# Decode step of the gated attention spread among the last gate projections, chunk 0's readout begun amid them, fourth plain weight in two tiles

## The chip, the cores and the metric

One core of one Trainium2 chip runs the whole step in one launch. The metric is the device time of that launch in microseconds; the profile is of one execution, and the times of the runs stand beside it.

## The reference

A decoder step of two layers for a prompt of 1024 tokens and 8 decode tokens, model width 1024. Cut to what this change touches, layer 0 is:

```python
h = rmsnorm(x, norm_mix_pre[l])
q, k, v, r, glr, qm = split_cols(h @ w_in_a[a], IN_A_SIZES)
g = log_sigmoid(glr @ w_gate_up[a] + b_gate[a]) / 16
o, S = gla_recurrence(q, k, v, g, gla_state[a])     # 4 heads, state 96 x 192 each
o_main = rmsnorm(o, gla_norm[a]) * silu(r)
o_mem = mem_attend(qm, mem_k[l], mem_v[l])
x = x + rmsnorm(concat([o_main, o_mem]) @ w_out[l], norm_mix_post[l])
f = square(relu(rmsnorm(x, norm_ffn_pre[l]) @ w_ffn_up[l])) @ w_ffn_down[l]
x = x + rmsnorm(f, norm_ffn_post[l])
```

For the 8 decode tokens the recurrence is a single step per head and token: the old state (an input, one per token) times exp(g), plus the outer product of k and v, is the new state (an output), and q times it is the token's o.

## The kernel before

The activations lie transposed, model width on partitions, and the 1032 tokens (1024 prompt, 8 decode) are three chunks of 384, 384 and 264 columns; the decode tokens are the last columns of chunk 2. Every float32 operand of a projection is split into a high and a low part (ScalarE's cast writes the high, VectorE's subtraction the low), and a projection of one 128-wide output block of one chunk, a *unit*, is 8 slices of the model width times three matmuls: high weight by high x, high by low, low by high, 24 in all (`proj`, lines 240 to 250). A unit's result is in one PSUM bank (tiles `mm`, `mx`); four banks go round.

Layer 0's mixer ends as follows. `in_r` (lines 1240 to 1265) runs the gate projections: for each unit VectorE takes the PSUM bank into a temporary `t` (L1257), clamps it (L1258), ScalarE takes exp, ln and exp (L1259 to L1261), VectorE makes r * silu(r) of it in three steps (L1262 to L1264), and SP's queue stores it to `srd` in DRAM (L1265). Blocks 0 to 2 run earlier, amid the prompt's recurrence. Blocks 3, 4 and 5, nine units, run last, chunk by chunk, with temporaries from a pool `gt` of four buffers.

The decode step of the recurrence stands in the program ahead of these nine units. For each of 4 heads SP loads the states `sin` and, broadcast, the v rows `vb`; for each of 8 tokens ScalarE scales a state (L1570) and VectorE adds k times v (L1571); SP stores the new states (L1572); 8 matmuls read them out into a PSUM tile `sf` or `sx` (L1577, 16 records, as each float32 matmul is recorded twice), and VectorE copies that to `vdec` (L1579). Then `vdec` is normed.

`out_proj` (from L487) follows: for chunk c, `make_o0` loads `srd` back (tile `sr`, L1592), transposes the recurrence's result block by block with TensorE (tile `ot`, two PSUM banks, L1595, 18 transposes for a 384-column chunk), multiplies both on VectorE (L1599) and splits the product into the operand `oh`/`ol` (records `xh<-sr`, `xl<-sr`). That operand lies in the buffers which chunk c of the layer's input had. Then 8 units per chunk with the weights `w_out`; the first three weights lie in the three buffers that hold the gate weights before.

The MLP (`mlp`, from L610) starts with four plain output blocks, m = 0 to 3, of each chunk (`up_plain`); three weights lie in the pool `wA`, the fourth (tile `wx`, both halves in one tile) in a pool `w4` on the side where the output weights lay.

A scheduling layer sets the order on each engine from the program's order, priorities and its own costs; engines then run their queues in order. So a step that moves in the program moves on five queues.

Of the kernel before, what the change touches and what calls it, by code (L numbers as in the profile page):

```python
# [8 lines left out]
F32 = mybir.dt.float32  # L9
F32R = mybir.dt.float32r  # L10
# [6 lines left out]
P = 128  # L17
D = 1024
KT = 8
# [9 lines left out]
DV = 192  # L29
# [4 lines left out]
NPL = 4  # L34
# [13 lines left out]
def hybrid_decoder_step(ctx: ExitStack, tc: tile.TileContext, A, O):  # L48
    nc = tc.nc
# [40 lines left out]
    def nm(s):  # L90
        uid[0] += 1
        return f"{s}_{uid[0]}"
# [35 lines left out]
    def stps(tag=None):  # L128
        turn[1] ^= 1
        tag = tag or ("sf", "sx")[turn[1]]  # L130
        return pst.tile([P, 512], F32, tag=tag, name=nm(tag))
# [105 lines left out]
        nc.gpsimd.tensor_tensor(ws, ws, gains[:, g, :].unsqueeze(2).to_broadcast([P, KT, P]), ALU.mult)  # L237
        nc.gpsimd.dma_start(wfd[i], ws)

    def proj(ps, w, hl, n, M=P, fine=False):  # L240
        wh, wl = w
        xh, xl = hl
        for k in range(KT):
            nc.tensor.matmul(ps[:M, :n], wh[:, k, :M], xh[:, k, :], start=(k == 0), stop=False)  # L244
            nc.tensor.matmul(ps[:M, :n], wh[:, k, :M], xl[:, k, :], start=False, stop=False)  # L245
            mm = nc.tensor.matmul(ps[:M, :n], wl[:, k, :M], xh[:, k, :], start=False, stop=(k == KT - 1))  # L246
            if fine:
                tick(mm, 3 * n)
        if not fine:
            tick(mm, 3 * KT * n)  # L250

    def xtiles(c):
        n = CH[c][1]
        h = xp.tile([P, KT, n], F32R, tag=f"xh{c}", name=nm("xh"))
        l = xp.tile([P, KT, n], F32R, tag=f"xl{c}", name=nm("xl"))
        return h, l
# [235 lines left out]
    def out_proj(l, make_o, src_pool, st, ff, xsrc, psum=True):  # L492
        wO = st.enter_context(tc.tile_pool(name=nm("wO"), bufs=5, reuse_waits="tile"))
        f0 = ff.pools[0]
        if psum:
            set_extra(st.enter_context(tc.tile_pool(name=nm("pmo"), bufs=2, space=PSUM, reuse_waits="tile")), 2)
        W = [wload(wA if m < 3 else wO, A["w_out"][l, m]) for m in range(KT)]
        OH, FT = {}, {}

        def prep(c):  # L500
            OH[c] = xtiles(c)
            make_o(c, OH[c])

        R = {}

        def part(c, ms, pool):
            n = CH[c][1]
            if c not in FT:
                FT[c] = pool.tile([P, KT, n], F32, tag="f", name=nm("f"))
                R[c] = Residual(c, FT[c], G_MIXPOST + l, xsrc, gnext=G_FFNPRE + l)  # L510
            for m in ms:
                ps = mmps()
                proj(ps, W[m], OH[c], n)
                with first():
                    nc.scalar.copy(FT[c][:, m, :], ps[:, :n])
# [96 lines left out]
    def mlp(l, X, ff):  # L612
        f = ff.f
        g = G_FFNPRE + l
# [6 lines left out]

        w4 = pool(left, "left", "w4")
        fa = pool(left, "left", "fa")
        w4s = pool_slot(w4, "w4")

        def plain_weights(src, homes, pri):
            W = []
# [10 lines left out]
        def up_plain(c):  # L638
            hl = X[c][0]
            c0, n = CH[c]  # L640
            for m in range(NPL):
                ps = mmps()
                proj(ps, W[m], hl, n)
                with first():
                    t = tmp3([P, 2, n])
                    nc.scalar.activation(t[:, 0, :], ps[:, :n], AF.Relu)
                    nc.scalar.activation(t[:, 1, :], t[:, 0, :], AF.Square)
                    nc.sync.dma_start(apd[l, :, m, c0 : c0 + n], t[:, 1, :])
# [379 lines left out]
    X = []  # L1028
# [86 lines left out]
    with ExitStack() as sl0:  # L1115
# [10 lines left out]
        with ExitStack() as sla:  # L1126
# [113 lines left out]
            def in_r(ms, staged=(), pool=None):  # L1240
                W = {m: wsplit(wA, staged[i]) if i < len(staged) else wload(wA, A["w_in_a"][12 + m])
                     for i, m in enumerate(ms)}
                for c, m in [(c, m) for c in range(3) for m in ms]:
                    w = W[m]
                    hl, r = X[c]
                    c0, n = CH[c]
                    ps = mmps()
                    proj(ps, w, hl, n)
                    if pool:
                        t = view(pool.tile([P, 768], F32, tag="t", name=nm("t")), [P, 2, n])  # L1250
                        y = pool.tile([P, 384], F32, tag="y", name=nm("y"))[:, :n]
                    else:
                        t = tmp3([P, 2, n])
                        y = view(tp.tile([P, 768], F32, tag="tq", name=nm("ry")), [P, n])
                    a, d = t[:, 0, :], t[:, 1, :]
                    with first():
                        TT(a, ps[:, :n], r, ALU.mult)  # L1257
                    nc.vector.tensor_scalar(d, a, -80.0, None, ALU.max)  # L1258
                    nc.scalar.activation(d, d, AF.Exp, scale=-1.0)  # L1259
                    nc.scalar.activation(y, d, AF.Ln, bias=oneb)  # L1260
                    nc.scalar.activation(y, y, AF.Exp, scale=-1.0)  # L1261
                    STT(d, d, 1.0, y, ALU.add, ALU.mult)  # L1262
                    STT(d, d, 2.0, y, ALU.subtract, ALU.mult)
                    STT(a, a, nglan[:, m : m + 1], d, ALU.mult, ALU.mult)  # L1264
                    nc.sync.dma_start(srd[:, m, c0 : c0 + n], a)  # L1265

            def head_norm(dst, src, rows, pool):
                nh = len(src)
# [286 lines left out]
        with ExitStack() as sd:  # L1555
            dp = sd.enter_context(tc.tile_pool(name="gdec", bufs=2, side="right", reuse_waits="tile"))
            d1 = sd.enter_context(tc.tile_pool(name="gdec1", bufs=1, side="right", reuse_waits="tile"))
            vdec = vdp.tile([P, 768], F32, tag="vdec", name="vdec")
            qmk = d1.tile([DK, H, NDEC, 32], F32, tag="qmk", name="qmk")
            nc.gpsimd.memset(qmk, 0.0)  # L1560
            for h in range(H):
                hv = slice(h * DV, h * DV + DV)
                sin = dp.tile([DK, NDEC, DV], F32, tag="sin", name=nm("sin"))
                nc.sync.dma_start(sin, A["state_gla"][:, h].rearrange("b k v -> k b v"))
                vb = dp.tile([DK, NDEC, DV], F32, tag="vb", name=nm("vb"))
                nc.sync.dma_start(vb, vdd[:, hv].unsqueeze(0).to_broadcast([DK, NDEC, DV]))
                for e in range(2):
                    nc.vector.tensor_copy(qmk[:, h, e::2, e], qd[:DK, QIDX[h], e::2])
                for bb in range(NDEC):
                    nc.scalar.mul(sin[:, bb, :], sin[:, bb, :], eg[:, h * NDEC + bb : h * NDEC + bb + 1])  # L1570
                    STT(sin[:, bb, :], vb[:, bb, :], qd[:DK, KIDX[h], bb : bb + 1], sin[:, bb, :], ALU.mult, ALU.add)  # L1571
                nc.sync.dma_start(O["sg_sample"][:, h].rearrange("b k v -> k b v"), sin)  # L1572
                ops = stps()
                row = Row()
                for e in range(2):
                    for g in range(4):
                        row(nc.tensor.matmul(ops[32 * g : 32 * g + 32, :DV], qmk[:, h, 2 * g + e, :],  # L1577
                                             sin[:, 2 * g + e, :], start=(e == 0), stop=(e == 1)))
                nc.vector.tensor_copy(vdec[:, hv], ops[:, :DV])  # L1579
            head_norm(vdec, [vdec[:, h * DV : h * DV + DV] for h in range(H)], P, d1)  # L1580

        ff = Sums()
        with ExitStack() as so:
# [16 lines left out]
                    split(oh[:, m, :], ol[:, m, :], sr)  # L1600
                split(oh[:, 6:8, :], ol[:, 6:8, :], qm[:, :, c0 : c0 + n])

            with tc.tile_pool(name="gt", bufs=4, reuse_waits="tile") as gt:
                in_r([3, 4, 5], pool=gt)
            X = out_proj(0, make_o0, svp, so, ff, A["xT"], False)
        pmd.close()

    X = mlp(0, X, ff)
# [377 lines left out]
```

## Time and profile before

| what | value |
|---|---|
| runs | 2226.27, 2228.89, 2230.83 us; median 2228.89 |
| profiled execution | 2224.17 us, span 2222.4 us |
| TensorE busy | 2161.7 us, 97% |
| VectorE busy | 1503.2 us, 68% |
| ScalarE busy | 1061.5 us, 48% |
| mean granted TensorE clock | 0.990 |

An engine's busy time is the sum of its instructions; TensorE's idle rest is 60.7 us. A wait is put down to the instruction that released it. Times in us count from the span's start; the nine gate units run from 351.86 to 408.

### The profile page before, as it was taken

The numbers are of one execution on the slowest core, as the hardware profiler recorded it, in microseconds if no ns is written. First come the engines' busy times: TensorE is split into PE (matmuls) and PEld (weight loads), VectorE is DVE, ScalarE is ACT, GpSimd is POOL, SyncE is SP. The second block draws the span as 40 slices with busy tenths as digits, with TensorE's granted clock in tenths as the row PEclk, the third lists the DMA queues.
The fourth block names the chain that finished last, engine by engine and source line by source line (L and its number), as shares of the span: only waits on it lengthen the run. The fifth ranks groups of instructions, "written<-read, shape, count | busy, mean of one in ns | idle before, by whom it ended". The sixth has DMA issues, their size and how long they took to land.

```text
span 2222.4 us, 40138 instructions
## 1 busy us (share of the span) xinstructions
PE 2161.7 (97%) x16250; PEld 2059.6 (93%) x16250; DVE 1503.2 (68%) x2811; ACT 1061.5 (48%) x2071; POOL 115.4 (5%) x123
## 2 busy tenths in 40 slices
PE   7999998999999999999999999899999999999997
PEld 5879997999999999999999878599999999999996
DVE  6656646758877777757569455647977777856557
ACT  6354534547554445333324355546755444433333
POOL 0002000000000001530000000200000000000010
PEclk9999999999999999999999999999999999999998
DMA  5412026434544449574324200415273346635422
GB/s 185 160 67 74 24 64 163 145 104 127 186 154 143 158 166 352 181 262 144 92 91 139 82 20 22 124 62 151 93 238 129 135 158 248 233 106 171 148 87 77
DMA packets 134687, 303.68 MB, mean 137 GB/s; under 512 B 11033, under 2 KB 65489, under 8 KB 134209
## 3 DMA queue, kind: packets, MB, share of 16 engines
q1 hardware_dynamic: 116736, 258.80, 35.7%
q0 software_dynamic: 7824, 29.44, 3.9%
q10 hardware_dynamic: 9936, 12.81, 1.6%
q8 instruction: 129, 2.11, 0.4%
q14 instruction: 62, 0.51, 0.1%
HBM read 213.57 MB, written 89.51 MB: 136 GB/s over the span
## 4 chain that ended last, share of the span: by engine, by line
PE 91%; DVE 4%; ACT 2%; DMA 1%; issue 1%; SPq 0%; DVEq 0%; ACTq 0%
PE mx L747 6%; PE mm L244 6%; PE mx L748 6%; PE mx L749 6%; PE mm L246 6%; PE mm L245 6%; PE mx L912 4%; PE mx L914 4%; PE mx L913 4%; PE mx L244 3%; PE mx L246 3%; PE mx L245 3%; PE mm L747 3%; PE mm L748 3%; PE mm L749 3%; PE mm L912 2%
## 5 line engine op out<-in xcount | busy, mean ns | idle before, releaser
L152 ACT CAST wh<-ws 128x512 fp32r<-128x512 f32 (+1 forms) x262 | 188.1, 726 | 319.3 <-DVE ws L600 107.2
L747 PE MATMUL mx<-xf,wh 128*128 128x258 f32 x1048 | 297.7, 284 | 0.0
L748 PE MATMUL mx<-xf,wh 128*128 128x258 f32 x1048 | 296.0, 282 | 0.0
L749 PE MATMUL mx<-xf,wl 128*128 128x258 f32 x1048 | 295.1, 282 | 0.0
L153 DVE TENSOR_TENSOR wl<-ws,wh 128x512 fp32r<-128x512 f32 (+1 forms) x262 | 213.4, 821 | 119.5 <-ACT wh L152 118.6
L244 PE MATMUL mm<-xh,wh 128*128 128x384 f32 (+1 forms) x864 | 281.5, 326 | 0.7 <-ACT xh L152 0.5
L246 PE MATMUL mm<-xh,wl 128*128 128x384 f32 (+1 forms) x864 | 279.0, 323 | 0.0
L245 PE MATMUL mm<-xl,wh 128*128 128x384 f32 (+1 forms) x864 | 278.4, 322 | 0.0
L152 ACT CAST wh<-wr 128x1024 fp32r<-128x1024 f32 x98 | 103.0, 1051 | 317.5 <-PE sx L913 302.0
L153 DVE TENSOR_TENSOR wl<-wr,wh 128x1024 fp32r<-128x1024 f32 x98 | 120.9, 1233 | 176.8 <-ACT wh L152 176.8
L912 PE MATMUL mx<-sa,wh 128*128 128x258 f32 x784 | 221.3, 283 | 0.0
L913 PE MATMUL mx<-sa,wh 128*128 128x258 f32 x784 | 220.5, 281 | 0.0
L914 PE MATMUL mx<-sa,wl 128*128 128x258 f32 x784 | 220.4, 281 | 0.0
L748 PEld LDWEIGHTS mx<-xf,wh 128*128 128x128 f32 x1048 | 198.0, 189 | 0.4
L747 PEld LDWEIGHTS mx<-xf,wh 128*128 128x128 f32 x1048 | 197.6, 189 | 0.4
L749 PEld LDWEIGHTS mx<-xf,wl 128*128 128x128 f32 x1048 | 197.9, 189 | 0.0
L244 PEld LDWEIGHTS mm<-xh,wh 128*128 128x128 f32 x864 | 163.0, 189 | 10.6 <-issue 6.7
L246 PEld LDWEIGHTS mm<-xh,wl 128*128 128x128 f32 x864 | 162.7, 188 | 7.3 <-issue 5.2
L245 PEld LDWEIGHTS mm<-xl,wh 128*128 128x128 f32 x864 | 163.1, 189 | 6.2 <-issue 4.7
L913 PEld LDWEIGHTS mx<-sa,wh 128*128 128x128 f32 x784 | 148.3, 189 | 0.0
L914 PEld LDWEIGHTS mx<-sa,wl 128*128 128x128 f32 x784 | 148.0, 189 | 0.0
L747 PE MATMUL mm<-xf,wh 128*128 128x258 f32 x520 | 147.6, 284 | 0.0
(546 smaller groups left out, 5769.9 us busy)
## 6 DMA issues: line engine op xcount, KB each, us to landing
ra<-awd SPq DMA_DIRECT2D x98, 516.0 KB, 3.7
ws<-in_w_up SPq DMA_DIRECT2D x64, 512.0 KB, 6.1
wr<-in_w_downb SPq DMA_DIRECT2D x56, 512.0 KB, 5.7
awd<-aw SPq DMA_DIRECT2D x26, 1032.0 KB, 6.8
awd<-am SPq DMA_DIRECT2D x28, 774.0 KB, 8.3
ws<-in_w_in_a SPq DMA_DIRECT2D x20, 512.0 KB, 3.8
xd<-f ACTq DMA_DIRECT2D x24, 384.0 KB, 4.7
ws<-in_w_out SPq DMA_DIRECT2D x16, 512.0 KB, 3.6
```

The source lines that it names most:

```text
L152: nc.scalar.copy(hi, src)
L153: (eng or nc.vector).tensor_tensor(lo, src, f32(hi), ALU.subtract)
L244: nc.tensor.matmul(ps[:M, :n], wh[:, k, :M], xh[:, k, :], start=(k == 0), stop=False)
L245: nc.tensor.matmul(ps[:M, :n], wh[:, k, :M], xl[:, k, :], start=False, stop=False)
L246: mm = nc.tensor.matmul(ps[:M, :n], wl[:, k, :M], xh[:, k, :], start=False, stop=(k == KT - 1))
L747: nc.tensor.matmul(ps, wh(k), xh, start=(k == 0), stop=False)
L748: nc.tensor.matmul(ps, wh(k), xl, start=False, stop=False)
L749: mm = nc.tensor.matmul(ps, wl(k), xh, start=False, stop=(k == n - 1))
L912: nc.tensor.matmul(ps, wh[:, q, ms], h, start=(jj == 0 and q == 0), stop=False)
L913: nc.tensor.matmul(ps, wh[:, q, ms], lo, start=False, stop=False)
L914: mm = nc.tensor.matmul(ps, wl[:, q, ms], h, start=False, stop=end)
```

## The change

The decode step becomes a generator, one step per head, and so do the gate units; behind units 1, 3, 5, 7 and 9 a loop runs one step of the decode. A head's readout is issued one step late, together with the next head's state update. After the sixth unit, chunk 0's operand of the output projection is made. The pools of the decode step now live beside the gate units, and the gate's temporaries have two buffers instead of four. In the MLP the fourth plain weight's high half lies in a new pool `w3` on the other side and its low half in `w4`; its units issue the 16 matmuls with the high half first and the 8 with the low half last.

```diff
-    def proj(ps, w, hl, n, M=P, fine=False):
+    def proj(ps, w, hl, n, M=P, fine=False, low_last=False):
...
+        terms = [(wh, xh), (wh, xl), (wl, xh)]
+        order = [(k, t) for k in range(KT) for t in terms]
+        if low_last:
+            order = [(k, t) for k in range(KT) for t in terms[:2]] + [(k, terms[2]) for k in range(KT)]
...
         def prep(c):
+            if c == 0 and oh0:
+                OH[c] = oh0
+                return
...
-        w4s = pool_slot(w4, "w4")
+        w3 = pool(ff.rest, "right", "w3")
+
+        def w4s():
+            return (w3.tile([P, KT, P], F32R, tag="wx", name=nm("wx")), w4.tile([P, KT, P], F32R, tag="w4", name=nm("wx")))
...
-                proj(ps, W[m], hl, n)
+                proj(ps, W[m], hl, n, low_last=(m == NPL - 1))
...
+            def r_units(ms, staged=(), pool=None):
...
                     nc.sync.dma_start(srd[:, m, c0 : c0 + n], a)
+                    yield
...
+        def gla_dec(dp, d1):
...
+                def readout(h=h, hv=hv, sin=sin):
...
+                if last:
+                    last()
+                last = readout
+                yield
+            last()
             head_norm(vdec, [vdec[:, h * DV : h * DV + DV] for h in range(H)], P, d1)
...
-            with tc.tile_pool(name="gt", bufs=4, reuse_waits="tile") as gt:
-                in_r([3, 4, 5], pool=gt)
-            X = out_proj(0, make_o0, svp, so, ff, A["xT"], False)
+            with ExitStack() as sd:
...
+                gt = sd.enter_context(tc.tile_pool(name="gt", bufs=2, reuse_waits="tile"))
+                dec = gla_dec(dp, d1)
+                for u, _ in enumerate(r_units([3, 4, 5], pool=gt)):
+                    if u % 2 == 0:
+                        next(dec, None)
+                    if u == 5:
+                        oh0 = xtiles(0)
+                        make_o0(0, oh0)
+            X = out_proj(0, make_o0, svp, so, ff, A["xT"], False, oh0)
```

What this does to TensorE's queue: before, between the fourth gate unit (`mm_5493`) and the fifth (`mx_5529`) stand twelve transposes, the readouts of heads 2 (`sin_5268`) and 3 (`sin_5301`) and three more transposes.

```order
L245 MATMUL mm_5493<-xl_191,wh_5369 128x384
L246 MATMUL mm_5493<-xh_190,wl_5370 128x384
L1595 MATMUL ot_5765<-ident,vtok 128x128 x3
L1595 MATMUL ot_5774<-ident,vtok 128x128 x3
L1595 MATMUL ot_5783<-ident,vtok 128x128 x3
L1595 MATMUL ot_5792<-ident,vtok 128x128 x3
L1577 MATMUL sx_5291<-sin_5268,qmk 32x192 x8
L1577 MATMUL sf_5324<-sin_5301,qmk 32x192 x8
L1595 MATMUL ot_5801<-ident,vtok 128x128 x3
L244 MATMUL mx_5529<-xh_190,wh_5375 128x384
```

Now, at the end of the seventh unit (`mm_5595`, chunk 2), the fourth block of transposes and then head 2's readout (`sin_5468`) stand between projections:

```order
L248 MATMUL mm_5595<-xl_249,wh_5214 128x264
L1616 MATMUL ot_5568<-ident,vtok 128x128 x3
L248 MATMUL mm_5595<-xh_248,wl_5215 128x264
L248 MATMUL mm_5595<-xh_248,wh_5214 128x264
L248 MATMUL mm_5595<-xl_249,wh_5214 128x264
L248 MATMUL mm_5595<-xh_248,wl_5215 128x264
L1592 MATMUL sx_5654<-sin_5468,qmk 32x192 x8
L248 MATMUL mm_5664<-xh_248,wh_5220 128x264
L248 MATMUL mm_5664<-xl_249,wh_5220 128x264
```

The readouts of heads 0 and 1 stand whole behind the third and the fifth unit, that of head 3 in four pieces among the first output-projection units. Transposes of chunk 0's blocks stand in and around the seventh to ninth unit, and twelve of chunk 1's in one run behind the third output-projection unit.

On VectorE, before, the updates of heads 2 and 3 stand whole ahead of the first instruction (L1257) of the first four units, whose banks are `mx_5385`, `mx_5421`, `mm_5457` and `mm_5493`:

```order
L1571 SCALAR_TENSOR_TENSOR sin_5268<-vb_5270,qd,sin_5268 96x192 x8
L1579 COPY vdec<-sx_5291 128x192
L1571 SCALAR_TENSOR_TENSOR sin_5301<-vb_5303,qd,sin_5301 96x192 x8
L153 TENSOR_TENSOR xl_5762<-sr_5772,xh_5761 128x384
L1579 COPY vdec<-sf_5324 128x192
L1599 TENSOR_TENSOR sr_5781<-ot_5783,sr_5781 128x384
L159 TENSOR_SCALAR sm_5341<-sm_5334 128x4
L153 TENSOR_TENSOR xl_5762<-sr_5781,xh_5761 128x384
L165 TENSOR_TENSOR sm_5342<-sm_5340 128x4
L166 SCALAR_TENSOR_TENSOR sm_5342<-sm_5342,sm_5341 128x4
L167 SCALAR_TENSOR_TENSOR sm_5340<-sm_5342,sm_5340 128x4
L1276 TENSOR_SCALAR vdec<-vdec,sm_5340 128x192 x4
```

(the four L1257 follow). Now the same steps of head 2 (`sin_5468`) stand among those of the fifth and sixth unit (`mx_5432`, `mx_5501`; the first instruction of a unit is L1270 in the new numbering):

```order
L1594 COPY vdec<-sf_5491 128x192
L1585 SCALAR_TENSOR_TENSOR sin_5468<-vb_5470,qd,sin_5468 96x192
L1270 TENSOR_TENSOR t_5457<-mx_5432,r_192 128x384
L1585 SCALAR_TENSOR_TENSOR sin_5468<-vb_5470,qd,sin_5468 96x192
L1271 TENSOR_SCALAR t_5457<-t_5457 128x384
L1585 SCALAR_TENSOR_TENSOR sin_5468<-vb_5470,qd,sin_5468 96x192 x6
L1270 TENSOR_TENSOR t_5526<-mx_5501,r_192 128x384
L1275 SCALAR_TENSOR_TENSOR t_5457<-t_5457,y_5458 128x384
```

So a unit's bank is emptied ahead of most of the next head's update. On ScalarE, before, the fourth plain weight's cast (`wx_6795`) stands behind the whole of chunk 0's second norm (`xh_6447`):

```order
L334 ACTIVATE xh_6447<-f_6218,gains 128x384
L515 COPY f_6490<-mm_6655 128x264
L328 DMA xd<-f_6218 128x2x384
L334 ACTIVATE xh_6447<-f_6218,gains 128x384 x2
L180 ACTIVATE tq_6652<-f_6490 128x528
L152 CAST wx_6795<-ws_6793 128x1024
L515 COPY f_6490<-mx_6681 128x264
```

Now it stands right behind the third weight's (`wh_6792`), ahead of that norm:

```order
L152 CAST wh_6792<-ws_6790 128x1024
L520 COPY f_6490<-mm_6545 128x264
L152 CAST wx_6798<-ws_6796 128x1024
L520 COPY f_6490<-mx_6571 128x264
L180 ACTIVATE tq_6597<-f_6490 128x528
L336 ACTIVATE xh_6447<-f_6218,gains 128x384
```

It moved from behind the norm to ahead of it. On TensorE, five matmuls with the fourth weight's high half now stand ahead of the other plain units, where there were two of that unit before.

More of the change, by code (lines that the diff above doesn't have):

```diff
@@ L238, in fold @@
         nc.gpsimd.dma_start(wfd[i], ws)
-    def proj(ps, w, hl, n, M=P, fine=False):
+    def proj(ps, w, hl, n, M=P, fine=False, low_last=False):
         wh, wl = w
         xh, xl = hl
[L243 to L247, printed above, removed]
+        terms = [(wh, xh), (wh, xl), (wl, xh)]
+        order = [(k, t) for k in range(KT) for t in terms]
+        if low_last:
+            order = [(k, t) for k in range(KT) for t in terms[:2]] + [(k, terms[2]) for k in range(KT)]
+        for i, (k, (w_, x_)) in enumerate(order):
+            mm = nc.tensor.matmul(ps[:M, :n], w_[:, k, :M], x_[:, k, :], start=(i == 0), stop=(i == 3 * KT - 1))
+            if fine and i % 3 == 2:
                 tick(mm, 3 * n)
@@ L490, in mem_dec_steps, with out_proj @@
                 nc.vector.tensor_copy(by_group(dq[rows, hp, :]), otv[rows, hp, :, h : h + 5 : 4])
-    def out_proj(l, make_o, src_pool, st, ff, xsrc, psum=True):
+    def out_proj(l, make_o, src_pool, st, ff, xsrc, psum=True, oh0=None):
         wO = st.enter_context(tc.tile_pool(name=nm("wO"), bufs=5, reuse_waits="tile"))
@@ L1238, in in_qm, with in_r @@
                     STT(qm[:, m, c0 : c0 + n], ps[:, :n], 0.125, r, ALU.mult, ALU.mult)
-            def in_r(ms, staged=(), pool=None):
+            def in_r(ms, staged=()):
+                for _ in r_units(ms, staged):
+                    pass
+            def r_units(ms, staged=(), pool=None):
                 W = {m: wsplit(wA, staged[i]) if i < len(staged) else wload(wA, A["w_in_a"][12 + m])
@@ L1554, in hybrid_decoder_step @@
         vdp = svp.enter_context(tc.tile_pool(name="vdec", bufs=1, side="right", reuse_waits="tile"))
[L1555 to L1558, printed above, removed]
+        vdec = vdp.tile([P, 768], F32, tag="vdec", name="vdec")
+        def gla_dec(dp, d1):
             qmk = d1.tile([DK, H, NDEC, 32], F32, tag="qmk", name="qmk")
             nc.gpsimd.memset(qmk, 0.0)
+            last = None
             for h in range(H):
@@ L1572, in hybrid_decoder_step @@
                 nc.sync.dma_start(O["sg_sample"][:, h].rearrange("b k v -> k b v"), sin)
[L1573 to L1579, printed above, removed]
+                def readout(h=h, hv=hv, sin=sin):
+                    ops = stps()
+                    row = Row()
+                    for e in range(2):
+                        for g in range(4):
+                            row(nc.tensor.matmul(ops[32 * g : 32 * g + 32, :DV], qmk[:, h, 2 * g + e, :],
+                                                 sin[:, 2 * g + e, :], start=(e == 0), stop=(e == 1)))
+                    nc.vector.tensor_copy(vdec[:, hv], ops[:, :DV])
+                if last:
[3 more added lines that the diff above has]
+            last()
             head_norm(vdec, [vdec[:, h * DV : h * DV + DV] for h in range(H)], P, d1)
@@ L1601, in make_o0 @@
                 split(oh[:, 6:8, :], ol[:, 6:8, :], qm[:, :, c0 : c0 + n])
-            with tc.tile_pool(name="gt", bufs=4, reuse_waits="tile") as gt:
-                in_r([3, 4, 5], pool=gt)
-            X = out_proj(0, make_o0, svp, so, ff, A["xT"], False)
+            with ExitStack() as sd:
+                dp = sd.enter_context(tc.tile_pool(name="gdec", bufs=2, side="right", reuse_waits="tile"))
+                d1 = sd.enter_context(tc.tile_pool(name="gdec1", bufs=1, side="right", reuse_waits="tile"))
+                gt = sd.enter_context(tc.tile_pool(name="gt", bufs=2, reuse_waits="tile"))
[7 more added lines that the diff above has]
+            X = out_proj(0, make_o0, svp, so, ff, A["xT"], False, oh0)
         pmd.close()
```

## The prediction

> **What bounds the kernel now.** I read the page first, then TensorE's waits by stretch, then its timeline where the waits cluster.
>
> ```profile
> span 2222.4 us, 40138 instructions
> ...
> PE 2161.7 (97%) x16250; PEld 2059.6 (93%) x16250; DVE 1503.2 (68%) x2811; ACT 1061.5 (48%) x2071; POOL 115.4 (5%) x123
> ```
>
> TensorE carries the time, so a change pays only by closing holes in it, and there are 60.7 us of them (2222.4 - 2161.7). The holes between 300 and 600 us are these (us in total, times, longest):
>
> ```profile
> PE ot L1595 <- DVE sr L1599: 2.7, 4, 1.2
> PE mm L244 <- ACT wx L152: 2.5, 1, 2.5
> PE mx L244 <- DVE t L1257: 2.1, 1, 2.1
> ...
> ```
>
> Everything here is at the seam that the diff touches. From 600 to 1200 us this view lists no wait at all, so a gain made here isn't lost in the first MLP. In time, the seam is:
>
> ```profile
> 374.67 0.34 PE L246 MATMUL mm<-xh,wl 128*128 128x384 f32 x1
> 374.86 0.82 PE L1595 MATMUL ot<-ident,vtok 128*128 128x128 f32 x6
> 375.99 1.01 PE L1595 MATMUL ot<-ident,vtok 128*128 128x128 f32 x6 [0.32 <-DVE sr L1599]
> 377.46 2.82 PE L1577 MATMUL sx<-sin,qmk 96*32 96x192 f32 x16 [0.46 <-DVE sin L1571]
> 381.05 3.46 PE L1577 MATMUL sf<-sin,qmk 96*32 96x192 f32 x16 [0.77 <-DVE sin L1571]
> 385.51 0.88 PE L1595 MATMUL ot<-ident,vtok 128*128 128x128 f32 x3 [1.01 <-DVE sr L1599]
> 388.54 0.69 PE L244 MATMUL mx<-xh,wh 128*128 128x384 f32 x1 [2.15 <-DVE t L1257]
> 389.02 0.52 PE L245 MATMUL mx<-xl,wh 128*128 128x384 f32 x1
> 389.34 0.52 PE L246 MATMUL mx<-xh,wl 128*128 128x384 f32 x1
> ...
> 394.23 0.34 PE L244 MATMUL mx<-xh,wh 128*128 128x384 f32 x1
> 394.41 0.33 PE L245 MATMUL mx<-xl,wh 128*128 128x384 f32 x1
> ```
>
> Four of the nine gate units have run by 374.86. Then no projection starts for 13.68 us, because VectorE, in its own order, takes the last two heads of the decode step before it empties the four PSUM banks:
>
> ```profile
> 376.99 2.71 DVE L1571 SCALAR_TENSOR_TENSOR sin<-vb,qd,sin 96x192 f32<-96x192 f32 x8
> 380.59 2.71 DVE L1571 SCALAR_TENSOR_TENSOR sin<-vb,qd,sin 96x192 f32<-96x192 f32 x8
> ...
> 387.93 1.01 DVE L1257 TENSOR_TENSOR t<-mx,r 128x384 f32<-128x384 f32 x2
> ```
>
> The named waits are short (0.32 to 2.15), but the loss is more than their sum. The matmuls after 388.54 start every 0.32 us (389.02 to 389.34) until 394.06, then every 0.18 (394.23 to 394.41). The granted clock says why (busy us of PE, PEld, DVE, ACT, POOL; PEclk; DMA):
>
> ```profile
> 375.00:380.00 5.00, 3.78 (x29) 1.75 (x26) 4.21 (x11) 4.03 (x12) 0.00 (x0) 1.00 0.64 133
> 380.00:385.00 5.00, 3.73 (x18) 1.09 (x16) 3.91 (x12) 2.77 (x10) 0.00 (x0) 0.53 0.60 157
> 388.54:394.06 5.52, 5.52 (x18) 5.52 (x19) 3.90 (x11) 3.89 (x9) 0.00 (x0) 0.51 0.01 4
> 394.06:424.60 30.54, 28.78 (x186) 27.58 (x186) 26.20 (x51) 17.36 (x33) 0.00 (x0) 1.00 0.47 151
> 424.60:440.00 15.40, 14.21 (x85) 13.73 (x84) 9.13 (x13) 7.78 (x13) 0.00 (x0) 1.00 0.67 212
> sum 88.14, PE 79.62 PEld 68.19 DVE 61.71 ACT 47.15 POOL 0.00; mean PE 15.92 PEld 13.64 DVE 12.34 ACT 9.43 POOL 0.00
> ```
>
> The sum row covers 351.86 (first gate unit) to 440.00 (sixth output-projection unit of chunk 0 done); I use it for VectorE's load below.
>
> **The seam, term by term.** *Decode spread out, readout one step late, transposes amid the units.* No matmul is added; they change places. The stretch 374.86 to 394.06 takes 19.20 us. What it must do at the full clock is 18 projection matmuls at 0.175 (394.23 to 394.41 and on) = 3.2, 32 readout records and 15 transposes. A readout record is priced from the first two heads, which in this trace already sit between projections:
>
> ```profile
> 367.21 0.84 PE L1577 MATMUL sf<-sin,qmk 96*32 96x192 f32 x10
> 367.98 0.44 PE L244 MATMUL mm<-xh,wh 128*128 128x384 f32 x1
> ```
>
> Ten take 0.77 from start to start, so 32 take 2.5; 15 transposes at 0.82/6 take 2.1. That leaves 19.2 - 7.8 = **11.4 us**, of which 2.5 is the half clock on 17 matmuls, 17 x (0.32 - 0.175). I take it as gone, since in the new order the readouts of heads 0 to 2 stand behind units 3, 5 and 7 and no PSUM bank has to wait: VectorE's first instruction of each unit now stands between the decode steps instead of behind them.
>
> *What is late next.* Walking the new orders with these durations, head 0's state is ready about 1.5 us before TensorE asks, heads 1 and 2 about 5 us; the third to sixth transposed blocks, whose two PSUM banks VectorE must empty, have a slack of 0.5 to 1 us. Head 3's readout and the fifth and sixth block of chunk 0's operand have none: they stand behind the split of the first output weights, which waits for the last gate units to leave their weight buffers. Each such handover can miss by about the 1.01 that the transposes wait at 385.51, or not at all. I charge 1.0.
>
> *The waits after 394.06.* TensorE idles 30.54 - 28.78 = 1.8 us and 15.40 - 14.21 = 1.2 in those two windows, on transposes and weight splits. The earlier start of chunk 0's operand can remove between nothing and all 3.0; the splits still hang on the last units, so I take half, **1.5**.
>
> *Two buffers for the gate's temporaries instead of four.* A unit's first VectorE instruction now waits until the store of the unit two before has landed. The nearest rows for the transfers (KB each, us to landing):
>
> ```profile
> sin<-in_state_gla SPq DMA_DIRECT2D x4, 576.0 KB, 6.8
> vb<-vdd SPq DMA_DIRECT2D x4, 576.0 KB, 6.6
> srd<-t SPq DMA_DIRECT2D x5, 192.0 KB, 3.0
> ```
>
> Two 384-column units occupy TensorE for 48 x 0.175 = 8.4 us; one unit's chain is five VectorE and three ScalarE steps of about 0.5 each, 4, plus 3.0 for the store. 7 fits under 8.4, and four PSUM banks give two further units of room. Zero, with that cover named.
>
> *DMA queue.* SP's queue now has the gate stores ahead of the state loads of heads 2 and 3, so SP waits for VectorE between them; the loads (6.8 and 6.6) were needed at 377 and have until about 385 and 393 now. Zero. The last state store leaves some 20 us later, and the second and third output weights queue behind gate stores; a weight has about 8 us between its load and its split. Zero. POOL's clearing of the mask tile stays where it is.
>
> **The fourth plain weight.** ScalarE casts it late, because its tile lay where output weights were still read:
>
> ```profile
> 508.98 0.28 PE L246 MATMUL mx<-xh,wl 128*128 128x264 f32 x1
> 511.74 0.44 PE L244 MATMUL mm<-xh,wx 128*128 128x384 f32 x1 [2.48 <-ACT wx L152]
> 490.55 7.51 SPq L223 DMA_DIRECT2D ws<-in_w_up  x3
> 495.61 0.37 ACT L515 COPY f<-mm 128x264 f32<-128x264 f32 x1
> 497.69 0.38 ACT L515 COPY f<-mx 128x264 f32<-128x264 f32 x1 [1.71 <-PE mx L246]
> 510.65 1.03 ACT L152 CAST wx<-ws 128x1024 fp32r<-128x1024 f32 x1
> DMA to landing us min/median/max: 3.4/3.4/3.5
> ```
>
> The weight is issued as the second of the three loads from 490.55, so it lands near 497. In the new order the cast stands between the copies of 495.61 and 497.69, where ScalarE idles 1.71, and costs it perhaps 0.3. Its low half, still split late, is read only after the 16 high matmuls. The wait goes: **2.5**, between 0 (if the operand's last slices, cast at 510, become the wait) and 2.5. The next thing TensorE needs is the sixth slice, after 5 + 18 matmuls or 4 us, at 513: late enough. The same edit in layer 1 has no wait to remove (one wx wait in the whole trace) and is zero, as is the order of the low matmuls elsewhere: same instructions.
>
> **The sum.** 11.4 + 1.5 + 2.5 - 1.0 = 14.4 us. The profiled execution took 2224.17 (span 2222.4), 4.7 below the median of the runs, 2228.89. The gain is an absolute one, so 2228.89 - 14.4 gives **2214.5**.
>
> **The clock, by row and by rule.** In this trace the clock fell near 380 although TensorE had idled at most 0.46 at a time since 374.86; it had done only transposes and readouts for 5 us. The Trainium skill, page "TensorE: Matmul & The Clock Gate", section "Why this matters for your kernels", asks for idle gaps of over about 3 us between matmul bursts for this; the trace differs, with gaps of 0.32 and 0.46. By that rule the new order, whose gaps are as short, could not lose clock, and the sum stands; by the row, 5 us without a projection is enough whatever the gaps. The same page, "Part 4: PE-mode transpose", says that transposes don't count as activity in the same way; the row at 380 agrees. The second rival is priced from the row alone.
>
> **Rivals.**
> - *VectorE takes over.* It has 61.7 us of work in the 88.14, and the stretch would shrink to 76.2 by the 11.9 us of the sum that aren't the weight: 81%. If it manages only 78% (it is at 70% now, and 26.20 of 30.54, 86%, in the window from 394), the stretch takes 79.1 and the gain is 9.0 + 2.5 = 11.5; at 73% (84.5) it is 6.1: 2217 to 2223. For it: nearly every handover is VectorE's. Against: the 86%.
> - *The clock falls again.* After chunk 0's first three output units, twelve transposes stand in one run, with waits for two banks among them. That is 12 x 0.14 + about 1 = 2.7 us without a projection, less than the 5 it took here. If it falls, 2.5 to 4.5 come back (17 matmuls, and readouts at 3.46 instead of 1.2): about 2218.
> - *It doesn't do what it says:* if the gate units and the decode step still serialize on VectorE, the holes move without shrinking and only the weight's 2.5 shows: 2226.
> - *Slower.* Two temporaries become a ring that everything passes. Besides the head's 8 steps, VectorE's queue has these in between (busy us, mean ns):
>
> ```profile
> L153 DVE TENSOR_TENSOR wl<-ws,wh 128x1024 fp32r<-128x1024 f32 x9 | 10.9, 1221 | 4.8 <-ACT wh L152 4.8
> L1599 DVE TENSOR_TENSOR sr<-ot,sr 128x384 f32<-128x384 f32 x12 | 6.5, 553 | 5.6 <-PE ot L1595 3.6 <-DMA sr<-srd 2.0
> ```
>
> If each pair of units takes the 7 above, a head (2.71), two operand blocks of two such steps and two weight splits (4 x 0.55 + 2 x 1.2), it is 14.3 instead of 8.4; four pairs cost 24 more, which is 9 over the 14.4: 2238. It decides only where the ring is over 3.6 us a pair longer than TensorE's 8.4, and TensorE has two spare banks before it feels it.
>
> **How the numbers follow.** Forecast (gain 10 to 20): 0.68, since the holes are plainly in the trace and the price doesn't rest on an unseen operation. VectorE takes over: 0.14. Clock: 0.07. No effect: 0.06. Slower: 0.05. About 0.2%, 4.5 us, can be told from no change; VectorE's case gives faster in all but a twentieth. Faster 0.88, same 0.07, slower 0.05. Range: the low end has no new wait and all of the waits regained, 11.4 + 3.0 + 2.5 = 16.9, and the 2.6 by which the lowest of the runs shown (2226.27) lies under their median: 2209, put at 2208.5; the high end is the end of VectorE's case, 2223.
>
> **What would show it.** Right: no readout record in a run of 32; no projection-free hole over 3 us between 350 and 400; granted clock 1.00 there; no wait on wx; TensorE's busy time nearly unchanged, its idle 9 to 14 lower. Wrong: a wait of transposes on sr or of readouts on sin of several us, first VectorE steps waiting on the store srd, or a clock under 1 after 400.

## The result, and the profile after

The changed kernel takes 2209.46 us (median of four runs, 2205.34 to 2210.11) against 2227.58 for the kernel before on the same chip (four runs, 2226.02 to 2230.83). The ratio is 0.9915, with a 95% interval of 0.9903 to 0.9928: 16.0 to 21.6 us faster, 18.1 by the medians. The forecast was 2214.5, range 2208.5 to 2223.0.

The profiled execution of the changed kernel took 2209.21 us, 15.0 less than that of the kernel before (2224.17), which was itself 3.4 under its kernel's median. The traces below divide these 15.0 us. Its page begins:

```profile
span 2207.4 us, 40137 instructions
...
PE 2152.1 (97%) x16250; PEld 2054.4 (93%) x16250; DVE 1504.0 (68%) x2811; ACT 1061.5 (48%) x2071; POOL 109.4 (5%) x123
```

TensorE is still the bound. For the same 16250 instructions its busy time is 9.6 us lower and its idle time 5.4 (60.7 to 55.3). Its waits between 300 and 600 us (us in total, times, longest) are down to two lines:

```profile
PE ot L1616 <- DVE sr L1620: 2.0, 3, 1.5
PE mx L248 <- ACT f L520: 1.0, 1, 1.0
```

The waits on wx and on t are gone; one on f, a copy of ScalarE's out of a PSUM bank, is new. In the changed kernel L248 is the projection matmul, L1592 the readout, L1616 the transposes, L1620 the sums that empty them, L1585 the state update, and L1270 a unit's first VectorE step. TensorE's timeline where the hole was:

```profile
365.55 0.34 PE L248 MATMUL mm<-xh,wl 128*128 128x384 f32 x1
365.82 0.86 PE L1592 MATMUL sx<-sin,qmk 96*32 96x192 f32 x16
366.61 0.44 PE L248 MATMUL mm<-xh,wh 128*128 128x384 f32 x1
...
384.29 0.55 PE L1616 MATMUL ot<-ident,vtok 128*128 128x128 f32 x3 [1.46 <-DVE sr L1620]
...
386.25 0.86 PE L1592 MATMUL sx<-sin,qmk 96*32 96x192 f32 x16
...
394.43 0.34 PE L248 MATMUL mx<-xl,wh 128*128 128x384 f32 x1
394.70 0.51 PE L1592 MATMUL sf<-sin,qmk 96*32 96x192 f32 x2
```

The readouts of heads 0 to 2 stand as single blocks of 16 records between projections (365.82, 375.13 and 386.25), some 10 us apart, with no wait ahead of them; head 3's begins in small pieces from 393.71 on. The one wait of over half a microsecond is at 384.29. The whole stretch, first gate unit to sixth output unit of chunk 0 (us; busy us and count of PE, PEld, DVE, ACT, POOL; granted clock; DMA share and GB/s):

```profile
353.11:425.83 72.72, 70.59 (x467) 64.89 (x465) 59.80 (x131) 47.08 (x105) 0.00 (x0) 1.00 0.72 200
```

The clock is 1.00 throughout, and VectorE works 82% of the time (59.80 of 72.72), where it was 70% of 88.14.

To see where the time came from, the same matmul is looked up in both timelines (the end of the seam is the first transpose of `vdec`, right behind chunk 0's sixth output unit). After:

```profile
353.24 0.34 PE L248 MATMUL mx<-xh,wh 128*128 128x384 f32 x1
425.83 0.29 PE L1618 MATMUL ot<-ident,vdec 128*128 128x8 f32 x2
494.68 0.34 PE L248 MATMUL mm<-xh,wx 128*128 128x384 f32 x1
541.42 0.28 PE L756 MATMUL mx<-xf,wh 128*128 128x258 f32 x1
2194.49 1.09 PE L198 MATMUL sf<-t,ones 128*128 128x264 f32 x2
```

Before (the first and third of the five are 351.86, the start of the first gate unit, and 511.74, the first matmul on wx, both told ahead):

```profile
440.11 0.29 PE L1597 MATMUL ot<-ident,vdec 128*128 128x8 f32 x2
557.33 0.28 PE L747 MATMUL mx<-xf,wh 128*128 128x258 f32 x1
2209.45 1.09 PE L198 MATMUL sf<-t,ones 128*128 128x264 f32 x2
```

| Stretch | before, us | after, us | gained |
|---|---|---|---|
| start to first gate unit | 351.86 | 353.24 | -1.4 |
| to chunk 0's sixth output unit (the seam) | 88.25 | 72.59 | 15.7 |
| to the first matmul on the fourth plain weight | 71.63 | 68.85 | 2.8 |
| to the first MLP product on xf | 45.59 | 46.74 | -1.1 |
| to the last matmul | 1652.12 | 1653.07 | -1.0 |

The first and last rows hold work that the change doesn't touch. So the change brings 17.3 us between the first gate unit and the first MLP product: 15.7 at the seam, and 1.6 at the weight, where 2.8 were gained and 1.1 given back to the new wait on f.

### The profile page after: what moved, and what is told of

The parts are those of the page before. It is cut to its first block, busy times and chain, and to the rows that moved or that the text cites. A ratio compares the mean times of both kernels' runs of the same rounds, so it can differ in the third digit from the quotient of the medians.

```text
span 2207.4 us, 40137 instructions
## 1 busy us (share of the span) xinstructions
PE 2152.1 (97%) x16250; PEld 2054.4 (93%) x16250; DVE 1504.0 (68%) x2811; ACT 1061.5 (48%) x2071; POOL 109.4 (5%) x123
## 4 chain that ended last, share of the span: by engine, by line
PE 84%; DVE 4%; ACT 2%; DMA 2%; issue 1%; DVEq 0%; ACTq 0%
PE mm L248 15%; PE mx L248 7%; PE mx L756 6%; PE mx L758 6%; PE mx L757 6%; PE mx L921 4%; PE mx L923 4%; PE mx L922 4%; PE mm L756 3%; PE mm L758 3%; PE mm L757 3%; PE mm L922 2%; PE mm L921 2%; PE mm L923 2%; PE sx L921 1%; PE sf L922 1%
## 5 line engine op out<-in xcount | busy, mean ns | idle before, releaser
L248 PE MATMUL mm<-xh,wh 128*128 128x384 f32 (+1 forms) x864 | 282.0, 326 | 0.8 <-ACT xh L152 0.5
L248 PE MATMUL mm<-xh,wl 128*128 128x384 f32 (+1 forms) x864 | 278.9, 323 | 0.0
L248 PE MATMUL mm<-xl,wh 128*128 128x384 f32 (+1 forms) x864 | 278.7, 323 | 0.0
L248 PEld LDWEIGHTS mm<-xh,wh 128*128 128x128 f32 x864 | 163.0, 189 | 10.8 <-issue 6.3
L248 PEld LDWEIGHTS mm<-xh,wl 128*128 128x128 f32 x864 | 162.6, 188 | 7.4 <-issue 5.4
L248 PEld LDWEIGHTS mm<-xl,wh 128*128 128x128 f32 x864 | 163.2, 189 | 6.5 <-issue 5.5
L921 PEld LDWEIGHTS mx<-sa,wh 128*128 128x128 f32 x784 | 147.5, 188 | 1.6 <-DVE aw L594 1.5
L922 PEld LDWEIGHTS mx<-sa,wh 128*128 128x128 f32 x784 | 148.4, 189 | 0.0
```

The costliest lines, as they stand in the source:

```text
L248: mm = nc.tensor.matmul(ps[:M, :n], w_[:, k, :M], x_[:, k, :], start=(i == 0), stop=(i == 3 * KT - 1))
L921: nc.tensor.matmul(ps, wh[:, q, ms], h, start=(jj == 0 and q == 0), stop=False)
L922: nc.tensor.matmul(ps, wh[:, q, ms], lo, start=False, stop=False)
```

## The experiments

Theory A: the hole is one of order; VectorE takes the last two heads' updates before it empties the gate units' PSUM banks, and spreading the decode removes it. Theory B: a large share comes from beginning chunk 0's operand early, which has TensorE and VectorE work ahead. Beside these: which half of the MLP edit removes the wait on wx, what the half clock is tied to, and whether two temporaries are the ring that the slower rival named.

All are timed against the kernel before, on the same chip within each group, so kernels of different groups are compared by their ratios, not by their medians. The last column is from the profiled execution alone: first gate unit to first MLP product, 205.5 us in the kernel before.

| Kernel | median, us | ratio (95%) | that stretch, us |
|---|---|---|---|
| changed kernel | 2209.46 | 0.9915 (0.9903-0.9928) | 188.2 |
| mlp_only | 2223.36 | 0.9985 (0.9975-0.9995) | 202.6 |
| seam_only | 2210.90 | 0.9931 (0.9918-0.9945) | 189.7 |
| no_early | 2211.20 | 0.9931 (0.9917-0.9946) | 191.5 |
| decode_last | 2215.71 | 0.9948 (0.9933-0.9964) | 194.5 |
| early3 | 2206.66 | 0.9916 (0.9897-0.9934) | 188.7 |
| early4 | 2207.66 | 0.9911 (0.9897-0.9926) | 186.6 |
| readout_now | 2211.70 | 0.9924 (0.9908-0.9940) | 194.6 |
| one_tile | 2210.80 | 0.9926 (0.9911-0.9942) | 191.0 |
| no_low_last | 2207.77 | 0.9914 (0.9895-0.9934) | 187.9 |
| gt1 | 2227.38 | 1.0004 (0.9990-1.0017) | 208.3 |
| filler | 2226.23 | 1.0005 (0.9992-1.0018) | 206.0 |

**The two parts apart.** mlp_only is the kernel before with the MLP edit alone; seam_only is the changed kernel without it:

```diff
-        w3 = pool(ff.rest, "right", "w3")
-        def w4s():
-            return (w3.tile([P, KT, P], F32R, tag="wx", name=nm("wx")), w4.tile([P, KT, P], F32R, tag="w4", name=nm("wx")))
+        w4s = pool_slot(w4, "w4")
...
-                proj(ps, W[m], hl, n, low_last=(m == NPL - 1))
+                proj(ps, W[m], hl, n)
```

> The kernel before with the MLP part alone: fourth plain weight in two tiles and its low half last, nothing moved at the seam. If the weight's wait is worth what the trace shows, the 2.5 us at the start of the plain units go and 1.1 of them come back as the wait on ScalarE's copy seen in the changed kernel: 1.5 us faster than before, about 2226. If the gain of the whole change lay in the MLP, it would be 10 us or more.

> The changed kernel with the MLP part taken back: decode step spread, chunk 0's operand early, weight as before. Theory: the seam carries nearly all, 15.5 us faster than before, about 2212, with the wait on wx of 2.5 still in the trace. Rival (the two parts need each other, the seam's gain waits at the fourth weight): under 12.

The seam alone gives 0.9931, 15.7 us off 2226.59; the MLP edit alone 0.9985, 3.2 us with an interval of 1.1 to 5.6. The parts add up to the whole within their intervals. In the trace of seam_only the wait on wx stands as it did (2.7 us, once). The gain is the seam's.

**Chunk 0's operand not begun early.** The changed kernel, with the operand left to the output projection:

```diff
-                    if u == 5:
-                        oh0 = xtiles(0)
-                        make_o0(0, oh0)
+            oh0 = None
```

> The changed kernel with chunk 0's operand made where it was made before, behind all nine units; the decode step stays spread. Theory A (the hole came from PSUM banks that VectorE emptied only behind the updates of heads 2 and 3): the nine units run without a hole and full clock, and only the 18 transposes with their waits, 3 to 5 us, come back: 2212 to 2215. Theory B (the gain is the early operand, transposes under projections): most of the gain goes, 2220 or more.

0.9931 against 0.9915: a sixth of a per cent by the ratios, and the intervals overlap. In the trace 3.3 us of the 17.3 go. The hole does not come back whole; a smaller one opens where the last head's readout meets its state update, and the clock dips behind it. TensorE's timeline and a window of no_early:

```profile
389.71 1.18 PE L1592 MATMUL sf<-sin,qmk 96*32 96x192 f32 x6
390.82 0.88 PE L1616 MATMUL ot<-ident,vtok 128*128 128x128 f32 x6
393.64 1.29 PE L1592 MATMUL sf<-sin,qmk 96*32 96x192 f32 x10 [1.95 <-DVE sin L1585]
```

```profile
395.00:400.00 5.00, 4.69 (x21) 3.82 (x22) 4.71 (x16) 3.38 (x11) 0.00 (x0) 0.77 0.80 259
```

Theory B as the main cause falls; the early operand is cover for the last head.

**The decode in one piece, behind the units.** The changed kernel, with the whole decode at the last unit:

```diff
-                    if u % 2 == 0:
-                        next(dec, None)
+                    if u == 8:
+                        for _ in dec:
+                            pass
```

> The changed kernel with the whole decode step issued behind the ninth gate unit instead of one step behind each other unit; the operand stays early. Theory A (it matters only that banks are emptied ahead of the decode updates): no hole among the units, 2209 to 2213. Theory C (the updates must be spread, because their 32 steps on VectorE and ScalarE in one run hold up what follows, now the first output weights' splits and the operand): a hole of 5 to 10 us behind the units instead, 2215 to 2220.

0.9948, with an interval clear of the changed kernel's. Two windows of decode_last, the seam whole and the place behind the units:

```profile
352.36:431.37 79.01, 74.29 (x465) 66.60 (x463) 61.53 (x134) 48.01 (x105) 0.00 (x0) 0.98 0.65 184
400.00:420.00 20.00, 16.98 (x91) 11.68 (x90) 14.72 (x39) 11.67 (x29) 0.00 (x0) 0.92 0.50 141
```

The seam takes 79.0 us, where the kernel before takes 88.25 and the changed kernel 72.6. So 9.2 of its 15.7 us, more than half, come without spreading the decode: no wait on t is left, since VectorE empties the gate units' banks first. (The operand is still made early in this kernel; both taken back together were not run.) The other 6.4 are lost behind the units, where the readouts of heads 2 and 3, in eight pieces, meet the output projection: 3.0 us idle between 400 and 420 and a clock of 0.92, where the changed kernel has 1.00. The time lies in Theory C's range; the trace has Theory A's sign, no hole among the units, and a loss behind them as Theory C has it. So the gain is split between the order on VectorE and the spreading.

**Where the operand begins, and the readout's delay.** early3 and early4 begin the operand after the fourth and the fifth unit (`u == 3`, `u == 4`); readout_now issues each readout in its own step:

```diff
-                if last:
-                    last()
-                last = readout
+                readout()
                 yield
-            last()
```

> The changed kernel with chunk 0's operand made behind the fourth gate unit instead of the sixth. If the wait of 1.5 us of the third block's transposes in the changed kernel comes from the operand's steps standing too late on VectorE, it goes and the time is 1 to 2 us under the changed kernel's. If VectorE is the bound there, the wait only moves to another handover: within 1 us of the changed kernel.

> The changed kernel with chunk 0's operand made behind the fifth gate unit; between the sixth (the changed kernel) and the fourth (measured as equal within the interval). If the place of the operand matters only through single handovers of about 1 us, it is equal to both within 2 us.

> The changed kernel with each head's readout issued with its own update, not one step late. If the delay is what keeps TensorE from waiting for VectorE's updates, waits on sin of 2 to 5 us appear, and pieces of readouts among projections at 0.27 us each add 2: 3 to 6 us slower than the changed kernel. If the scheduling layer moves the readouts back anyway, within 2 us.

The place is indifferent: 0.9916 and 0.9911 beside 0.9915. In early3 the wait on f isn't there and those on sr grow from 2.0 to 3.4 us in total; what one handover gains another loses. readout_now's stretch is 6.4 us longer, without any wait on the state update. Its timeline shows what it has more of: a readout's matmuls, each of which reads one token's state, stand in pieces between projections:

```profile
371.81 0.34 PE L248 MATMUL mm<-xh,wh 128*128 128x384 f32 x1
372.08 0.53 PE L1592 MATMUL sf<-sin,qmk 96*32 96x192 f32 x8
372.54 0.45 PE L248 MATMUL mm<-xl,wh 128*128 128x384 f32 x1
...
384.05 0.34 PE L248 MATMUL mx<-xh,wl 128*128 128x384 f32 x1
384.32 0.51 PE L1592 MATMUL sx<-sin,qmk 96*32 96x192 f32 x2
384.76 0.45 PE L248 MATMUL mx<-xh,wh 128*128 128x384 f32 x1
385.05 0.34 PE L248 MATMUL mx<-xl,wh 128*128 128x384 f32 x1
```

From projection to projection a piece of two records takes 0.71 us and one of eight 0.73, of which 0.175 is the projection: 0.54 and 0.56 for the piece. A whole readout takes 1.06 (365.55 to 366.61 after), 0.89 for 16 records. Sixteen pieces instead of seven cost 3.9 of the 6.4 (fifteen at 0.54 and one of ten records at 0.87, 9.0, against 5.1 after). The projection right behind a piece also starts its successor later, 0.29 us (384.76 to 385.05) instead of 0.175: 0.1 for each of nine more pieces, 1.0. TensorE's idle time in the seam, 3.2 against 2.1, is another 1.1. By the timed ratio, 0.9924, it is only 2.0 us slower than the changed kernel, and the intervals overlap. In this profiled execution the work from the first MLP product to the last matmul took 4.8 us less than in the changed kernel's; the runs don't explain that.

**The fourth plain weight.** one_tile keeps the new matmul order and takes the two tiles back (`w4s = pool_slot(w4, "w4")`); no_low_last keeps the tiles and takes the order back (a `proj` without `low_last`):

> The changed kernel with the fourth plain weight back in one tile of the old pool; its matmuls stay in the new order, low half last. If the wait went because the high half's tile lies where nothing is still read, it is back (2.5 us on wx, and the 1.1 on ScalarE's copy goes): 1.5 us slower than the changed kernel, about 14 to 16 under before. If the order of the matmuls did it, no change.

> The changed kernel with the fourth plain weight's matmuls in the old order, high and low mixed; two tiles stay. If two tiles alone bring the early cast, the wait on wx stays away and the time is the changed kernel's within 1 us; if the low half, split late, becomes the wait, it is 1 to 2.5 us slower.

TensorE's waits in one_tile, then in no_low_last:

```profile
PE mm L248 <- ACT wx L152: 2.5, 1, 2.5
```

```profile
PE mx L248 <- ACT f L520: 0.9, 1, 0.9
```

The tiles alone remove the wait; the order does nothing that these runs can tell (0.9914). The wait on f appears only in kernels with two tiles (though not in early3, early4 and gt1). ScalarE's timeline in the changed kernel:

```profile
494.78 1.12 ACT L336 ACTIVATE xh<-f,gains 128x384 fp32r<-128x384 f32 x2 [1.57 <-DVE f L327]
...
496.34 0.36 ACT L520 COPY f<-mx 128x264 f32<-128x264 f32 x1
```

The copy that empties an output unit's bank (496.34) stands behind the norm, which itself waits 1.57 for VectorE. While TensorE waited for wx, a late copy here cost nothing, as seam_only and one_tile show, which have the wait on wx and not this one.

**One temporary instead of two** (`name="gt", bufs=1`), for the slower rival:

> The changed kernel with one buffer for the gate's temporaries instead of two. The rival of the prediction that ended slower, driven on purpose: each unit's first VectorE step then waits for the store of the unit just before, a ring of 4 us of steps and 3 us of store against 4.2 us of matmuls. If the ring can bind, 10 to 20 us are lost against the changed kernel and the waits name srd; if the four PSUM banks and the later slack take it up, under 4 us are lost, and two buffers had much room.

1.0004: the whole gain is gone. TensorE's waits in gt1:

```profile
PE mx L248 <- ACT wh L152: 7.3, 1, 7.3
PE ot L1616 <- DVE sr L1620: 6.1, 6, 2.4
PE mx L248 <- DVE t L1270: 2.7, 1, 2.7
PE ot L1616 <- DVE sm L165: 2.1, 1, 2.1
PE mm L248 <- DVE t L1270: 0.9, 1, 0.9
```

and the casts behind the first of them, from ScalarE's timeline:

```profile
434.18 1.99 ACT L152 CAST wh<-ws 128x1024 fp32r<-128x1024 f32 x2 [2.32 <-DMA srd<-t]
```

The ring that I had in mind, a unit's first step behind a store, shows as the two lines on t, 3.6 us. More goes where I had not looked: the cast of an output weight waits for a store out of the temporaries, so the units' lag reaches the weights, and the transposes' handovers grow from 2.0 to 6.1. The clock, too, is at 0.91 over the 91.5 us from the first gate unit on (353.49 to 445). VectorE itself waits for the stores 2.0 us in all between 340 and 440, hardly more than the 1.4 with two buffers, in the changed kernel, where TensorE has no wait on t:

```profile
DVE t L1270 <- DMA srd<-t: 1.4, 2, 1.1
```

So little of the loss is VectorE standing at a store. The smaller pool also changed the order of the queues (head 3's readout stands in other pieces and places), and the runs don't take the two apart.

**What the half clock is tied to.** filler is the kernel before, with twelve additional matmuls of 256 columns behind each of the readouts of heads 2 and 3, whose results nothing uses:

```diff
+                if h >= 2:
+                    xf = X[2][0][0]
+                    for k in range(12):
+                        row(nc.tensor.matmul(ops[:, 256:512], xf[:, k % KT, :P], xf[:, k % KT, :256],
+                                             start=(k == 0), stop=(k == 11)))
```

> The kernel before with 24 extra matmuls of 256 columns whose result nobody reads, 12 behind the readout of head 2 and 12 behind that of head 3, in the middle of the hole; about 2.8 us more work for TensorE. If the clock fell because TensorE did no projection for 5 us, it now stays at 1.00 there, the matmuls behind the hole start every 0.175 us at once (2.5 us regained), and the time is about that of before, 2 us either way. If the clock falls for another reason, it falls all the same and the time is 2 to 4 us above before.

Its time is the same as before, 1.0005. Windows of filler, and its timeline (L1582 are the extra matmuls):

```profile
380.00:385.00 5.00, 4.33 (x30) 2.22 (x29) 3.46 (x12) 3.95 (x13) 0.00 (x0) 1.00 0.46 123
385.00:390.00 5.00, 2.79 (x25) 2.08 (x25) 3.07 (x11) 1.38 (x5) 0.00 (x0) 1.00 0.46 121
390.00:395.00 5.00, 4.35 (x16) 4.35 (x17) 3.75 (x12) 2.02 (x5) 0.00 (x0) 0.66 0.00 2
```

```profile
381.31 1.69 PE L1582 MATMUL sx<-xh 128*128 128x256 f32 x12
...
383.78 2.16 PE L1577 MATMUL sf<-sin,qmk 96*32 96x192 f32 x14 [0.33 <-DVE sin L1571]
385.87 1.69 PE L1582 MATMUL sf<-xh 128*128 128x256 f32 x12
...
390.65 0.59 PE L244 MATMUL mx<-xh,wh 128*128 128x384 f32 x1 [2.76 <-DVE t L1257]
391.04 0.52 PE L245 MATMUL mx<-xl,wh 128*128 128x384 f32 x1
```

In the kernel before, the clock was 0.53 in 380 to 385 and 0.51 from 388.54 to 394.06. With projection-like work behind each of the two readouts it holds 1.00 to 390 and falls only behind the wait of 2.76. Pauses don't tell the two apart: ahead of the fall in before none was longer than 0.46, and filler has 0.32, 0.45 and 0.33 in the same place.

But filler doesn't settle it either. In before the fall came at 380.3, and filler, about 1.1 us later at this place, had got there with the clock at 1.00 before its first extra matmul at 381.31. The clock's records change only at steps that lie 3.413 us apart, so the stretch that ends at a step is what has to be compared. Two of them ended in a fall although TensorE was busy most of the time: in before 376.9 to 380.3, with 2.8 us of readouts and 0.1 of transposes, and in mlp_only, whose seam is that of before, 378.3 to 381.7, with 2.6 us of readouts and no transpose. Three kept 1.00 with hardly a projection: filler's 377.1 to 380.6 (1.0 us of transposes, 2.0 of readouts), mlp_only's 374.9 to 378.3 (1.0 and 1.7) and decode_last's 410.1 to 413.5 (2.0 and 0.8), which begins with one transpose and ten readout records and goes on with these:

```profile
411.09 0.77 PE L1616 MATMUL ot<-ident,vtok 128*128 128x128 f32 x5
412.18 1.01 PE L1616 MATMUL ot<-ident,vtok 128*128 128x128 f32 x6 [0.32 <-DVE sr L1620]
```

The other falls between 340 and 520 in all the traces (filler, no_early, decode_last, gt1, one_tile) end stretches with 1.9 us or more of pauses, and no stretch with so much kept 1.00. So it matters how a wait lies to the steps: the wait on wx (2.48 in before, 2.46 in one_tile) put 1.8 us into one stretch in before, which kept 1.00, and 2.2 in one_tile, where the clock fell. So in these traces the clock fell behind readouts with short pauses or behind long pauses, and stretches with 1.0 us of transposes or more among the readouts held it. This is read from a few stretches; no run varies the readouts alone. The Trainium skill, page "TensorE: Matmul & The Clock Gate", section "Part 4: PE-mode transpose", says that transposes don't count as busy in the same way; decode_last's stretch doesn't bear that out. Its section "Why this matters for your kernels", by which the clock needs idle gaps of more than about 3 us to fall, doesn't fit before's row, where 0.46 was the longest.

The time doesn't change although the clock holds longer. The two blocks of extra matmuls cost 1.6 and 1.5 us, and the hole stays, since VectorE's order is as it was: 14.7 us from the first transposes to 390.65, before 13.7. Behind it eleven matmuls still run at the half clock, where before had seventeen; the 2.5 us that I expected back came only to 0.9. So filler doesn't price the half clock. What stands for its price is the sum from the rows of before, 2.5 us on seventeen matmuls, a small part of the seam's 15.7.

## Why the prediction was right

The direction, the cause and the place came out as written, and the time lies in the range, 5.0 us under the forecast and 1.0 above the low end of the range. Of the 5.0, 1.3 are the base (2228.89 by the three runs shown, 2227.58 by the four of the comparison). The rest is partly what the change gained, partly which executions were profiled: the traces are 15.0 us apart, the medians 18.1. Term by term, against the traces:

- *The hole, 11.4 and 1.5, less 1.0 for tight handovers: 11.9 predicted, 15.7 measured.* This is the term that was mis-sized. Its cause was right (seam_only, decode_last). The size failed at the readouts, in two places. I priced 32 records of heads 2 and 3 at 2.5 by the rate of a piece of ten, and left the pieces of heads 0 and 1 as they were. In before each of those two readouts was cut into pieces of 2, 2, 2 and 10 records:

```profile
361.77 0.34 PE L245 MATMUL mx<-xl,wh 128*128 128x384 f32 x1
362.04 0.84 PE L1577 MATMUL sx<-sin,qmk 96*32 96x192 f32 x10
362.81 0.44 PE L246 MATMUL mx<-xh,wl 128*128 128x384 f32 x1
363.09 0.34 PE L244 MATMUL mx<-xh,wh 128*128 128x384 f32 x1
363.36 0.51 PE L1577 MATMUL sf<-sin,qmk 96*32 96x192 f32 x2
363.80 0.44 PE L245 MATMUL mx<-xl,wh 128*128 128x384 f32 x1
```

  From projection to projection, less 0.175, that is 0.87 for the ten and 0.54 for each two: 2.5 for a readout in pieces, 5.0 for the two heads, to which one wait for issue adds 0.4. After, both stand whole at 0.89 each, 1.8, since the readout is issued one step late, when the whole state is ready: 3.6 more gained. Against that, head 2 is whole (0.9) and head 3 in pieces (2.5), 3.4 where I had 2.5. Net 2.7 of the missing 3.8. The sum also took 18 projections off a stretch that holds 17 (0.2). I had quoted the piece of ten and read its price as a rate per record; it is mostly a price per piece.
- *The handovers.* I left 2.5 us of waits in the stretch (1.5 of the 3.0 kept, 1.0 new). Idle there is 2.1 (72.72 - 70.59), 1.46 of it at 384.29, among the third to sixth transposed blocks, where I had given them 0.5 to 1 of slack. So the charge was near its size, 0.4 too high, but the miss came at the third block, which I had given slack, and not at the handovers without any: that part was luck. The last 0.5 of the difference I can't assign.
- *The fourth plain weight, 2.5: 2.8 gained, 1.1 given back.* The wait on wx went, and a wait that I had not named came: ScalarE's copy behind the norm. I looked for what TensorE needs next among weights and operand slices, and not among the banks that the delayed ScalarE must empty.
- *Two temporaries and the store queue, zero.* Right, by a small margin: VectorE's waits on the stores are 1.4 us, and gt1 shows that one buffer fewer costs the whole gain.
- *VectorE takes over.* I had it at 81% in 76.2 us; it did 82% in 72.72. The limit that this rival supposed at 78% isn't there.
- *The clock falls again.* Not in the changed kernel's seam. In no_early and decode_last, where the blocks close up again, it does for one short window, behind stretches with 1.9 and 2.4 us of pauses. My reading of the row at 380, 5 us of transposes and readouts without a projection, was too simple: the run of transposes that I priced as a danger stands in decode_last, and the clock held through it.
- *The signs to look for.* No run of 32 readout records, no projection-free hole over 3 us, the clock at 1.00 and no wait on wx: as written. "Busy nearly unchanged, idle 9 to 14 lower" was wrong: idle fell 5.4 and busy 9.6. Matmuls at half clock fill 0.32 us each instead of 0.175 and count as busy all the while, and much of a piece's changeover counts as busy too (0.51 for two records), so a loss of this sort shows in busy time as much as in idle time.

## What to carry to other kernels

When two engines hand work back and forth, read the order on the engine that empties the PSUM banks before that on TensorE: putting the short steps that free banks ahead of a long independent chain gave 9.2 of the seam's 15.7 us without interleaving the decode. Price small groups of matmuls from the starts of the projections around them, not from busy time or per record, and issue them whole. When a wait goes, look at every queue of the engine that released it for what becomes late next, and compare starts of the same instruction in both traces; sums of idle time mislead.

## What the runs showed of the hardware

- A group of narrow float32 readouts between projections costs 0.54 to 0.56 us whether it has two records or eight, and 0.87 to 0.89 with ten or sixteen (the rows of readout_now, before and after above), and 0.1 more at the projection behind it (0.29 from 384.76 to 385.05, against 0.175). I had priced it by the record.
- The clock fell to half behind 3.4 us of almost nothing but readouts, with no pause over 0.46 us (before, at 380.3), or no pause over 0.77 (mlp_only, at 381.7). It held through 2.0 us of transposes and 0.8 of readouts (decode_last, up to 413.5). Between 340 and 520 it fell behind every stretch between two steps with 1.9 us or more of pauses (no_early, filler, decode_last, gt1, one_tile), and behind none with 1.8 or less but the two of readouts.
- By the clock's records the half rate in the seam lasted 13.65 us in before (380.3 to 393.9), 10.24 in mlp_only, and 3.41 in filler, no_early and decode_last, once in each. The first is four times the last, as the Trainium skill, page "TensorE: Matmul & The Clock Gate", section "What's actually happening", has it with a free-running window of 3413 ns. The 361.8 us of full clock ahead of before's fall are 106 such windows.
